# One more PE tap group, a bias table sent from POOL's queue, splits ahead of squares and a layer normalisation on PSUM rows, in a two-layer encoder

## The chip, the cores and the metric

One core of one Trainium2 chip. The metric is the device time of one execution in microseconds (us); before the change its median is 2296.82 us over 3 runs. Engines: PE (TensorE) multiplies matrices, DVE (VectorE), ACT (ScalarE) and POOL (GpSimd) work element by element, and SP (SyncE) only issues DMAs. ACT and POOL can issue DMAs too. Each engine takes its instructions in the order of its own queue, and waits at the head of it.

## The reference, cut to what matters

```python
def _conformer_conv(h, w_in, b_in, dw_w, dw_b, ln_g, ln_b, w_out, b_out):
    u = h @ w_in + b_in
    a, gate = jnp.split(u, 2, axis=-1)
    u = a * jax.nn.sigmoid(gate)
    u = _causal_dwconv(u, dw_w, dw_b)            # 31 taps on each channel
    u = jax.nn.silu(_layernorm(u, ln_g, ln_b))   # over the 2048 channels
    return u @ w_out + b_out

def reference(x, ...):                           # x: 256 positions x 2048 channels
    for i in range(2):
        h = _rmsnorm(x, mix_norm[i])
        m = _conformer_conv(h, ...) if i == 0 else _diff_attention(h, ...)
        x = x + m
        h = _rmsnorm(x, ffn_norm[i])
        x = x + _conv_ffn(h, ...)                # up, 3 taps, silu gate, down
    return _rmsnorm(x, final_norm_g)
```

The attention adds to its scores a bias that depends on the distance of key and query through a table of 32 buckets for each of 16 heads, and masks keys of later chunks of 64.

## The kernel before

Channels lie on the 128 partitions, the 256 positions along the free dimension. Every weight arrives as a 512 KB chunk of f32 (`load_w`, L140, SP's queue, 5 buffers), ACT rounds it to a high part (`split_w`, L150, 6 buffers) and DVE or POOL forms the low part (L152, 6 buffers); PE multiplies high and low parts. A list of steps, one chunk each, is run in order (`run`); `ahead` keeps the splits up to four chunks ahead of PE, and `at(d, fn)` emits `fn` d steps later. The order that reaches the engines' queues is not quite that of the text: a scheduler goes through the program with modelled times, and gives an engine whichever instruction is ready, the earliest in the text first. So a wait that the model takes for short can stand ahead of other work on its queue. Inside `manual_schedule` the order of the text is kept.

**Start** (`setup`). The 8 tiles of x are split for the first product (`split_act`, L267 on ACT and L268 on DVE), four weight splits stand between them, and behind each tile its square is added to a sum on DVE (`x_square`, L321). Then `norm_cols` and `norm_rows` make the reciprocal norms (one small POOL instruction, L286; `rstd`, L348).

**Convolution** (`conv_module`). 16 channel tiles, each 4 chunks of `w_in`; from tile 2 on POOL forms all low parts. After a tile's product `post` scales it (L436, PSUM to an SBUF tile E), ACT takes the sigmoid (L438), DVE makes the gated u (L440). ACT sends u to DRAM (`ud`, L452) and fetches it back in four shifted copies R (L456). On PE, `taps` does the first 4*G taps of the channel with R and diagonals that POOL builds (`dg`, L458; G is 2 groups for tiles 0 to 10, 3 for 11 and 12, 5, 6 and 0 for the last ones); it is emitted 4 steps behind `post`. DVE does the other taps one by one (`tap_step`, L513, at most 6 a step), and `dev` (L544) takes the deviation; POOL sums deviations and squares (L559, L560), for tile 13 DVE. The last tile has 18 taps on PE out of its own tile (`last_taps`, L484) with diagonals built at the start (L466, POOL).

**Layer normalisation** (`layernorm`, in front of the first step of `w_out`). The statistics become two rows (`rows`, L280, in PSUM) which ACT copies to SBUF (L599); DVE (pairs 0, 1, 3, 5, 7) and POOL (2, 4, 6) multiply and subtract them in place (L607, L608, L611), ACT applies Silu (L615) and rounds (L617), DVE forms the low part (L621), and PE starts on `w_out` pair by pair.

**Bias table** (`attn_setup`, emitted at the first step of the first feed-forward part). A small product gives the bias of each head and distance (L730, 16 partitions), and a DMA from ACT's queue writes it 128 times into DRAM (`d1`, L732, 3 MB). In the attention each head's 128x256 window of it is fetched by ACT (`bias`, L809) and masked by POOL (L810). The norm of the first feed-forward part (L285 DVE, L286 POOL, L280 PE, L348 ACT) is emitted just behind `attn_setup`.

Of the kernel before, what the change touches and what calls it, by code (L numbers as in the profile page):

```python
# [8 lines left out]
F32 = mybir.dt.float32  # L9
# [52 lines left out]
class Builder:  # L62
# [79 lines left out]
    def split_w(self):  # L142
# [9 lines left out]
        eng.tensor_tensor(lo[:, :n], raw[:, :n], hi[:, :n].bitcast(F32), ALU.subtract)  # L152
# [42 lines left out]
    def step(self, src, n, cols, mm, post=None, pre=None, lo="v"):  # L195
# [4 lines left out]
        self.steps.append(dict(w=wi, mm=mm, post=post, pre=pre))  # L200

# [177 lines left out]
    def setup(self, n0):  # L379
# [46 lines left out]
    def conv_module(self, nin, nout):  # L426
# [6 lines left out]
        def post(i, ps):  # L433
            with self.tc.high_priority():
                t = self.b2("E")
                nc.vector.tensor_tensor(t, ps[:, :, 0:S], nin["rstd"].unsqueeze(1).to_broadcast([P, 2, S]), ALU.mult)  # L436
# [20 lines left out]
            dg = self.ph1.tile([P, 4 * gm, 32], F32, tag="dg", name=self.nm("dg"))[:, :4 * g, :]  # L457
            nc.gpsimd.tensor_tensor(dg, self.cmask.unsqueeze(1).to_broadcast([P, 4 * g, 32]),  # L458
                                    self.col("wq", 4 * sum(c.G[:i]), 4 * g).unsqueeze(2).to_broadcast([P, 4 * g, 32]), ALU.mult)
            self.at(4, lambda: taps(i, u, R, dg))  # L460
# [78 lines left out]
        def dev(i, acc, rest=None):  # L539
# [7 lines left out]
            if i < KT - 2:  # L547
# [4 lines left out]
                eng = nc.gpsimd if i < KT - 3 else nc.vector  # L552
# [25 lines left out]
        def layernorm():  # L578
# [21 lines left out]
            bc = [rs[:, x, :].unsqueeze(1).to_broadcast([P, 2, S]) for x in range(2)]  # L600
            pools = [pr for pr in range(2, KT // 2) if pr % 2 == 0]

            def norm(pr, part):
                d = D[pr][1]
                if pr == 0:
                    d = d[:, part, :]
                    nc.vector.tensor_tensor(d, d, rs[:, 0, :], ALU.mult)  # L607
                    nc.vector.tensor_tensor(d, d, rs[:, 1, :], ALU.subtract)  # L608
                    return
                eng = nc.gpsimd if pr in pools else nc.vector  # L610
                eng.tensor_tensor(d, d, bc[part], ALU.mult if part == 0 else ALU.subtract)  # L611
# [7 lines left out]
            def low(i):  # L619
                h = hh[i][1]  # L620
                nc.vector.tensor_tensor(h[:, 1, :], D[i // 2][1][:, i % 2, :], h[:, 0, :].bitcast(F32), ALU.subtract)  # L621

            with self.tc.manual_schedule(engines={ET.DVE, ET.Activation, ET.Pool}):
                dve = [pr for pr in range(KT // 2) if pr not in pools]
                todo = [(pr, part) for pr in dve for part in range(2)]
                for x in todo[:2]:
                    norm(*x)
                todo = todo[2:]
                for pr in pools:
                    norm(pr, 0)  # L630
                    norm(pr, 1)
                for i in range(KT):

                    while todo and 2 * todo[0][0] + todo[0][1] <= i + 2:
                        norm(*todo.pop(0))
                    act(i)
                    if todo and i >= 1:
                        norm(*todo.pop(0))
                    low(i)
# [8 lines left out]
        for pr in range(KT // 2):  # L648
            def post2(ps, pr=pr):
                self.x_add(ps, pr, bias="bout")  # L650
                self.x_done(nout, pr)
                if pr == KT // 2 - 1:
                    self.free(hh.values())
                    self.norm_later(nout)
            off = self.pair(a["w_out"], off, c.kcs, lambda k: hh[k], post2, pre=layernorm if pr == 0 else None,
                            lo="g" if pr < 2 else "v")

# [61 lines left out]
    def attn_setup(self):  # L719
# [4 lines left out]
        nc.scalar.dma_start(rb, a["relb"])  # L724
        oh = self.b2("Z").rearrange("p a s -> p (a s)")[:NB, :384]
        nc.scalar.dma_start(oh, a["oneh"])
# [22 lines left out]
    def attention(self, nin, nout):  # L749
# [3 lines left out]
        V, U, O = {}, {}, {}  # L753
# [52 lines left out]
        def bias(h):  # L806
            bm = self.ph2.tile([P, S], F32, tag="bm", name=self.nm("bm"), bufs=2)
            o = h * P * 384 + P - 1
            nc.scalar.dma_start(bm, self.bflat[o:o + P * 383].rearrange("(p d) -> p d", d=383)[:, :S])  # L809
            nc.gpsimd.memset(bm[0:64, S - 64:], MASK)  # L810
            return bm

        def scores(h, q, k, qk):
            bm = bias(h)
# [67 lines left out]
        for h in range(H):  # L882
            if h % 4 == 0:
                voff = v_group(h // 4, voff)
            off = self.pair(a["w_qk"], off, c.kcs, lambda k: nin["xh"][k], lambda ps, h=h: qk_post(h, ps))
# [149 lines left out]
```

## Time and profile before

| | us |
|---|---|
| median of 3 runs (2295.39 to 2298.47) | 2296.82 |
| the profiled execution | 2303.02 |
| its span, first to last instruction | 2300.4 |
| PE busy in the span | 2224.6 |

Names such as L475 are lines of the kernel. `out<-in` names the tiles that an instruction writes and reads. In a timeline the bracket behind an instruction tells how long its engine stood idle before it, and what it waited for. PE's clock has two levels, 1.2 and 2.4 GHz; the profile gives the granted one as a share of the higher.

### The profile page before, as it was taken

To read this page: it belongs to the slowest core of one execution; us is meant where nothing else is said; L and a number is where in the kernel's file an instruction comes from. 1 tells how busy PE (TensorE), PEld (TensorE's weight loads), DVE (VectorE), ACT (ScalarE), POOL (GpSimd) and SP (SyncE) were. 2 spreads that over 40 slices of the span, in tenths; PEclk is the share of its full clock that TensorE was granted. 3 is DMA by queue.
4 is the path that set the end of the run, shared out by engine and by line. 5 is a ranking of instruction groups with operands and counts; after the bars stand their busy time and mean duration, and the time that the engine had idled before them with its cause. 6 is when DMAs were issued, how large, how long until landed. Compare 5 with 4: busy or idle time off the path is not lost.

```text
span 2300.4 us, 34637 instructions
## 1 busy us (share of the span) xinstructions
PE 2224.6 (97%) x13294; PEld 1947.9 (85%) x13294; DVE 1670.9 (73%) x2539; ACT 1205.7 (52%) x1788; POOL 281.4 (12%) x189
## 2 busy tenths in 40 slices
PE   6899799799999999999999999999999999999998
PEld 6788688688888888888888888888888888888887
DVE  5788876577777767677766777677777777676774
ACT  5333265455555555455655555555555555554554
POOL 5678510000000000000111011010000000000002
PEclk9999899899999999999999999999999999999999
DMA  6766356766666666666655555466666666666663
GB/s 230 195 193 190 111 159 179 191 198 187 190 188 188 187 188 190 188 190 188 188 179 159 168 168 166 140 200 183 189 188 190 186 190 185 191 187 190 189 187 100
DMA packets 126885, 417.15 MB, mean 181 GB/s; under 512 B 14176, under 2 KB 28288, under 8 KB 126720
## 3 DMA queue, kind: packets, MB, share of 16 engines
q1 hardware_dynamic: 110736, 398.30, 56.8%
q10 hardware_dynamic: 15984, 16.65, 3.5%
q8 instruction: 104, 1.70, 0.3%
q14 instruction: 61, 0.50, 0.1%
HBM read 407.44 MB, written 7.45 MB: 180 GB/s over the span
## 4 chain that ended last, share of the span: by engine, by line
PE 88%; DMA 5%; DVE 4%; issue 1%; ACTq 0%; ACT 0%; POOL 0%; POOLq 0%; SPq 0%; DVEq 0%
PE pp L226 47%; PE pp L227 24%; PE pp L224 4%; PE pp L217 3%; PE pp L223 2%; DMA R<-ud 2%; DMA ud<-cpad 2%; DMA d<-Z 2%; PE pp L774 1%; PE pp L775 1%; PE pp L776 1%; DVE s L513 1%; DVE cpad L440 1%; PE s L475 0%; ACTq L456 0%
## 5 line engine op out<-in xcount | busy, mean ns | idle before, releaser
L226 PE MATMUL pp<-act,hi 128*128 128x512 f32 x3902 | 1382.9, 396 | 21.1 <-DVE E L256 13.0
L227 PE MATMUL pp<-act,lo 128*128 128x256 f32 x3902 | 1096.5, 281 | 0.0
L150 ACT CAST hi<-raw 128x1024 fp32r<-128x1024 f32 x752 | 787.6, 1049 | 536.0 <-PE pp L226 179.3
L152 DVE TENSOR_TENSOR lo<-raw,hi 128x1024 fp32r<-128x1024 f32 x686 | 844.3, 1231 | 283.0 <-ACT hi L150 281.2
L226 PEld LDWEIGHTS pp<-act,hi 128*128 128x128 f32 x3902 | 733.3, 188 | 182.9 <-DVE E L256 13.3
L227 PEld LDWEIGHTS pp<-act,lo 128*128 128x128 f32 x3902 | 739.1, 189 | 10.4
L226 PE MATMUL pp<-actb,hi 128*128 128x512 f32 x856 | 306.7, 396 | 0.0
L227 PE MATMUL pp<-actb,lo 128*128 128x256 f32 x856 | 240.4, 281 | 0.0
L321 POOL TENSOR_TENSOR ssq<-ssq,Z 128x512 f32<-128x512 f32 x24 | 35.6, 1481 | 1532.1 <-ACT Z L317 1532.0
L217 PE MATMUL pp<-act,hi 128*128 128x256 f32 x1088 | 209.3, 294 | 11.4 <-ACT act L267 6.0
L217 PEld LDWEIGHTS pp<-act,hi 128*128 128x128 f32 x1088 | 178.0, 200 | 19.3 <-DVE act L268 6.6
L226 PEld LDWEIGHTS pp<-actb,hi 128*128 128x128 f32 x856 | 160.6, 188 | 38.3 <-issue 0.6
L152 POOL TENSOR_TENSOR lo<-raw,hi 128x1024 fp32r<-128x1024 f32 x66 | 159.4, 2434 | 56.0 <-ACT hi L150 52.4
L256 DVE TENSOR_TENSOR E<-pp,E 128x512 f32<-128x512 f32 x104 | 71.8, 690 | 128.2 <-ACT E L254 127.9
L227 PEld LDWEIGHTS pp<-actb,lo 128*128 128x128 f32 x856 | 161.5, 189 | 0.2
L217 PE MATMUL pp<-act,lo 128*128 128x256 f32 x544 | 158.4, 291 | 2.8 <-DVE lo L152 2.8
L254 ACT COPY E<-pp 128x512 f32<-128x512 f32 x104 | 60.8, 585 | 186.9 <-PE pp L224 161.6
L370 ACT COPY E<-pp 128x512 f32<-128x512 f32 x109 | 63.9, 586 | 169.5 <-PE pp L224 161.8
L677 DVE SCALAR_TENSOR_TENSOR Y<-fpad,prm,Y 128x256 f32<-128x256 f32 x352 | 146.7, 477 | 0.0
L372 DVE TENSOR_TENSOR x<-pp,x 128x512 f32<-128x512 f32 x101 | 69.7, 690 | 89.4 <-ACT E L370 89.0
L674 ACT ACTIVATE Y<-fpad,prm 128x256 f32<-128x256 f32 x176 | 96.3, 596 | 48.2 <-DVE fpad L670 48.2
L513 DVE SCALAR_TENSOR_TENSOR s<-cpad,cprm,s 128x256 f32<-128x256 f32 x214 | 97.5, 482 | 24.8 <-PE s L475 22.6
(218 smaller groups left out, 1890.8 us busy)
## 6 DMA issues: line engine op xcount, KB each, us to landing
raw<-in_w_up_dram SPq DMA_DIRECT2D x352, 512.0 KB, 4.0
raw<-in_w_down_dram SPq DMA_DIRECT2D x176, 512.0 KB, 4.0
raw<-in_w_in_dram SPq DMA_DIRECT2D x64, 512.0 KB, 4.5
raw<-in_w_qk_dram SPq DMA_DIRECT2D x64, 512.0 KB, 3.6
raw<-in_w_out_dram SPq DMA_DIRECT2D x32, 512.0 KB, 4.1
raw<-in_w_v_dram SPq DMA_DIRECT2D x32, 512.0 KB, 3.7
raw<-in_w_o_dram SPq DMA_DIRECT2D x32, 512.0 KB, 3.7
R<-ud ACTq DMA_DIRECT2D x44, 130.0 KB, 5.1
```

Source lines behind the costliest of these rows:

```text
L150: nc.scalar.copy(hi[:, :n], raw[:, :n])
L152: eng.tensor_tensor(lo[:, :n], raw[:, :n], hi[:, :n].bitcast(F32), ALU.subtract)
L217: nc.tensor.matmul(ps[:, 0:S], w[:, kk, cs], xt[:, x, :], start=(k == first and n == 0), stop=(k == last and n == 2))
L224: nc.tensor.matmul(*main, start=False, stop=True)
L226: nc.tensor.matmul(*main, start=(k == first), stop=False)
L227: nc.tensor.matmul(*corr, start=False, stop=False)
L256: nc.vector.tensor_tensor(t, ps[:, :, 0:S], cs, ALU.add)
L370: nc.scalar.copy(cs, ps[:, :, S:])
L372: nc.vector.tensor_tensor(x, ps[:, :, 0:S], x, ALU.add)
L513: nc.vector.scalar_tensor_tensor(acc, u[:, j:j + S], self.col("cw", i * CK + j), acc, ALU.mult, ALU.add)
L674: nc.scalar.activation(y[:, j, :], u[:, j, FK - 1:], AF.Identity, scale=self.col("fw", ch * FK + FK - 1), bias=self.col("fb", ch))
L677: nc.vector.scalar_tensor_tensor(y[:, j, :], u[:, j, q:q + S], self.col("fw", ch * FK + q), y[:, j, :], ALU.mult, ALU.add)
```

## The change

- `G` becomes 3 for tiles 0 to 12: for tiles 0 to 10 PE does 12 taps in place of 8, DVE 19 in place of 23. `taps` is emitted 5 steps behind `post` for tiles 0 to 13, 4 for tile 14.
- `post` works in place in PSUM: no SBUF tile E, and the PSUM buffer is held until u is made.
- The diagonals of tile 0 and of the last tile are queued on POOL behind the last low part emitted so far.
- `setup` does all splits of x and the first four weight splits, and only then the squares, with two more weight splits between them.
- All sums of deviations and squares go to POOL, two folds for tile 14 also.
- `layernorm`: DVE reads the two rows from PSUM, POOL alone uses the SBUF copy, pair 0 is done by halves first, Silu writes PSUM tiles, and the steps of the first two output pairs alternate.
- `attn_setup`: the three DMAs leave from POOL's queue, and 16 small ones (64 x 64 values each) write the mask into the table behind it. `bias` is fetched from SP's queue, ahead of the head's product, with no masking afterwards.

```diff
-        self.G = [2] * (self.KT - 5) + [3, 3, 5, 6, 0]
+        self.G = [3] * (self.KT - 3) + [5, 6, 0]
...
+    def interleave(self, s0):
+        st = self.steps[s0:]
+        n, w0 = len(st) // 2, st[0]["w"]
+        st = [x for ab in zip(st[:n], st[n:]) for x in ab]
+        self.W[w0:] = [self.W[x["w"]] for x in st]
...
                     self.split_act(n0["xh"][m][1], self.X[pr][:, j, :], self.col("mixg", m))
+
+            for pr in range(KT // 2):
+                if pr % 3 == 2:
+                    self.ahead(4 + pr // 3)
                 self.x_square(n0, pr, nc.vector)
...
-                t = self.b2("E")
-                nc.vector.tensor_tensor(t, ps[:, :, 0:S], nin["rstd"].unsqueeze(1).to_broadcast([P, 2, S]), ALU.mult)
+                t = ps[:, :, 0:S]
+                nc.vector.tensor_tensor(t, t, nin["rstd"].unsqueeze(1).to_broadcast([P, 2, S]), ALU.mult)
...
+            queue = self.tc.issue_after(self.pool_lo) if i == 0 else ExitStack()
+            with queue:
+                diagonals(i, g, dg)
+            self.at(5 if i < KT - 2 else 4, lambda: taps(i, u, R, dg))
...
-                eng = nc.gpsimd if i < KT - 3 else nc.vector
+                eng = nc.gpsimd
...
-                    nc.vector.tensor_tensor(h[x], src[:, 0, :], src[:, 1, :], ALU.add)
+                    nc.gpsimd.tensor_tensor(h[x], src[:, 0, :], src[:, 1, :], ALU.add)
...
+            rp = [self.psx("s", [P, S]) for _ in range(2)]
             rs = self.b2("E")
             for x, v in enumerate((rc, mr)):
-                ps = self.psx("s", [P, S])
-                self.rows(ps, v)
-                nc.scalar.copy(rs[:, x, :], ps)
+                self.rows(rp[x], v)
...
+                if j is not None:
+                    nc.vector.tensor_tensor(d[:, j, :], d[:, j, :], rp[part], ops[part])
+                elif pr in pools:
+                    nc.gpsimd.tensor_tensor(d, d, rs[:, part, :].unsqueeze(1).to_broadcast([P, 2, S]), ops[part])
+                else:
+                    nc.vector.tensor_tensor(d, d, rp[part].unsqueeze(1).to_broadcast([P, 2, S]), ops[part])
...
             def act(i):
-                z = D[i // 2][1][:, i % 2, :]
-                nc.scalar.activation(z, z, AF.Silu, scale=self.col("lng", i), bias=self.col("lnb", i))
+                z = self.psx("to"[i % 2], [P, S])
+                nc.scalar.activation(z, D[i // 2][1][:, i % 2, :], AF.Silu, scale=self.col("lng", i),
+                                     bias=self.col("lnb", i))
...
+                for j in range(2):
+                    norm(0, 0, j)
+                    norm(0, 1, j)
+                for x in range(2):
+                    nc.scalar.copy(rs[:, x, :], rp[x])
...
+            if pr == 1:
+                self.interleave(s0)
...
-        nc.scalar.dma_start(rb, a["relb"])
+        nc.gpsimd.dma_start(rb, a["relb"])
...
-        nc.scalar.dma_start(d1, tb.unsqueeze(1).to_broadcast([H, P, 384]))
+        nc.gpsimd.dma_start(d1, tb.unsqueeze(1).to_broadcast([H, P, 384]))
         self.bflat = d1.rearrange("h p d -> (h p d)")
+
+        mk = self.ph2.tile([64, 64], F32, name="mk")
+        nc.gpsimd.memset(mk, MASK)
+        for h in range(H):
+            o = h * P * 384 + P - 1
+            nc.gpsimd.dma_start(self.bflat[o:o + 64 * 383].rearrange("(p d) -> p d", d=383)[:, S - 64:S], mk)
...
         def bias(h):
-            bm = self.ph2.tile([P, S], F32, tag="bm", name=self.nm("bm"), bufs=2)
+            BM[h] = self.ph2.tile([P, S], F32, tag="bm", name=self.nm("bm"), bufs=2)
             o = h * P * 384 + P - 1
-            nc.scalar.dma_start(bm, self.bflat[o:o + P * 383].rearrange("(p d) -> p d", d=383)[:, :S])
-            nc.gpsimd.memset(bm[0:64, S - 64:], MASK)
-            return bm
+            d = nc.sync.dma_start(BM[h], self.bflat[o:o + P * 383].rearrange("(p d) -> p d", d=383)[:, :S])
+            self.tc.keep_in_program_order(d)
```

## Rows read from the trace of the kernel before

**Rows 1.** PE's waits, whole span: who waited for whom, us, times, longest.
```profile
PE s L475 <- DMA R<-ud: 14.0, 7, 4.9
PE pp L226 <- DVE E L256: 13.0, 1, 13.0
...
PE t L475 <- DMA R<-ud: 6.0, 3, 2.6
...
PE s L484 <- DVE cpad L440: 3.8, 1, 3.8
```

**Rows 2.** Stretches: length, then busy time of PE, PEld, DVE, ACT, POOL, clock, DMA.
```profile
450.00:1150.00 700.00, 700.00 (x4007) 613.16 (x4006) 519.99 (x694) 386.64 (x527) 10.49 (x7) 1.00 0.63 190
```

**Rows 3.** DVE's timeline at the start: start, us, operation.
```profile
30.45 1.21 DVE L152 TENSOR_TENSOR lo<-raw,hi 128x1024 fp32r<-128x1024 f32 x1
```

**Rows 4.** POOL's timeline at the start.
```profile
38.27 14.56 POOL L152 TENSOR_TENSOR lo<-raw,hi 128x1024 fp32r<-128x1024 f32 x6
```

**Rows 5.** DVE's timeline, `post` of tiles 3 and 14: L436 starts as their product ends.
```profile
79.83 0.68 DVE L436 TENSOR_TENSOR E<-pp,rstd 128x512 f32<-128x512 f32 x1
...
239.51 0.68 DVE L436 TENSOR_TENSOR E<-pp,rstd 128x512 f32<-128x512 f32 x1
```

**Rows 6.** The chain that ended last, tiles 11 to 13: start, us, what.
```profile
195.81 0.59 DVE E L436
...
198.63 1.10 PE s L475 x16
...
201.20 5.07 DMA ud<-cpad
...
207.67 5.00 DMA R<-ud
...
212.80 1.50 PE t L475 x24
214.30 11.72 PE pp L217 x96
```

**Rows 7.** POOL's groups, first 300 us: busy us, mean ns, idle before.
```profile
L152 POOL TENSOR_TENSOR lo<-raw,hi 128x1024 fp32r<-128x1024 f32 x66 | 159.4, 2434 | 56.0 <-ACT hi L150 52.4 <-DMA raw<-in_w_in_dram 3.6
...
L560 POOL TENSOR_TENSOR lnsq<-lnsq,Z 128x512 f32<-128x512 f32 x5 | 6.4, 1287 | 0.0
...
L458 POOL TENSOR_TENSOR dg<-cmask,cprm 128x384 f32<-128x384 f32 x2 | 1.9, 928 | 0.0
```

**Rows 8.** DVE's timeline, end of the convolution and layer normalisation.
```profile
257.06 2.60 DVE L568 TENSOR_TENSOR M<-act 128x256 f32<-128x256 f32 x1
...
262.07 0.68 DVE L436 TENSOR_TENSOR E<-pp,rstd 128x512 f32<-128x512 f32 x1
...
280.56 1.48 DVE L607 TENSOR_TENSOR act<-act,E 128x256 f32<-128x256 f32 x1
...
288.71 0.41 DVE L621 TENSOR_TENSOR act<-act,act 128x256 fp32r<-128x256 f32 x1
```

**Rows 9.** PE's timeline around the layer normalisation.
```profile
277.66 1.16 PE L280 MATMUL s<-ident,c 128*128 128x128 f32 x8 [1.51 <-POOL c L593]
286.56 0.80 PE L226 MATMUL pp<-act,hi 128*128 128x512 f32 x1 [7.75 <-DVE act L621]
```

**Rows 10.** ACT's timeline: a Silu, and the start of the feed-forward part.
```profile
288.23 0.60 ACT L615 ACTIVATE act<-act,prm 128x256 f32<-128x256 f32 x1 [3.71 <-DVE act L611]
...
427.82 0.59 ACT L254 COPY E<-pp 128x512 f32<-128x512 f32 x1 [25.08 <-DMA d<-Z]
```

**Rows 11.** POOL's and PE's timelines there.
```profile
400.90 0.70 POOL L286 TENSOR_TENSOR rc<-c,mhalf 128x2 f32<-128x2 f32 x1 [25.41 <-DVE c L285]
...
404.97 0.61 PE L280 MATMUL o<-ident,rc 128*128 128x128 f32 x4
```

**Rows 12.** Weight loads issued from 390 to 430 us: count, landing min/median/max.
```profile
L140 SPq DMA_DIRECT2D raw<-in_w_up_dram x5: 327/2642/4511, 390.9 to 404.7; - x5
...
DMA to landing us min/median/max: 4.5/18.2/18.7
```

More of the change, by code (lines that the diff above doesn't have):

```diff
@@ L151, in split_w @@
         eng = nc.gpsimd if w["lo_eng"] == "g" else nc.vector
-        eng.tensor_tensor(lo[:, :n], raw[:, :n], hi[:, :n].bitcast(F32), ALU.subtract)
+        ins = eng.tensor_tensor(lo[:, :n], raw[:, :n], hi[:, :n].bitcast(F32), ALU.subtract)
+        if w["lo_eng"] == "g":
+            self.pool_lo = ins.ins
         w["hi"] = hi[:, :n].rearrange("p (k c) -> p k c", c=w["cols"])
@@ L200, in step @@
         self.steps.append(dict(w=wi, mm=mm, post=post, pre=pre))
+    def interleave(self, s0):
[3 more added lines that the diff above has]
+        self.W[w0:] = [self.W[x["w"]] for x in st]
+        for i, x in enumerate(st):
+            x["w"] = w0 + i
+        self.steps[s0:] = st
     def pair(self, wsrc, off, ksub, src, post, lo="v", pre=None, held=None, merged=False, halves=None):
@@ L457, in post, with diagonals @@
             dg = self.ph1.tile([P, 4 * gm, 32], F32, tag="dg", name=self.nm("dg"))[:, :4 * g, :]
+            queue = self.tc.issue_after(self.pool_lo) if i == 0 else ExitStack()
+            with queue:
+                diagonals(i, g, dg)
+            self.at(5 if i < KT - 2 else 4, lambda: taps(i, u, R, dg))
+        def diagonals(i, g, dg):
             nc.gpsimd.tensor_tensor(dg, self.cmask.unsqueeze(1).to_broadcast([P, 4 * g, 32]),
                                     self.col("wq", 4 * sum(c.G[:i]), 4 * g).unsqueeze(2).to_broadcast([P, 4 * g, 32]), ALU.mult)
-            self.at(4, lambda: taps(i, u, R, dg))
             if i == 0:
@@ L594, in layernorm @@
             nc.vector.tensor_tensor(mr, mean, rc, ALU.mult)
+            rp = [self.psx("s", [P, S]) for _ in range(2)]
             rs = self.b2("E")
             for x, v in enumerate((rc, mr)):
-                ps = self.psx("s", [P, S])
-                self.rows(ps, v)
-                nc.scalar.copy(rs[:, x, :], ps)
-            bc = [rs[:, x, :].unsqueeze(1).to_broadcast([P, 2, S]) for x in range(2)]
+                self.rows(rp[x], v)
             pools = [pr for pr in range(2, KT // 2) if pr % 2 == 0]
-            def norm(pr, part):
+            ops = (ALU.mult, ALU.subtract)
@@ L604, in norm @@
+            def norm(pr, part, j=None):
                 d = D[pr][1]
[L605 to L611, printed above, removed]
+                if j is not None:
[4 more added lines that the diff above has]
+                    nc.vector.tensor_tensor(d, d, rp[part].unsqueeze(1).to_broadcast([P, 2, S]), ops[part])
@@ L613, in act @@
             def act(i):
-                z = D[i // 2][1][:, i % 2, :]
-                nc.scalar.activation(z, z, AF.Silu, scale=self.col("lng", i), bias=self.col("lnb", i))
+                z = self.psx("to"[i % 2], [P, S])
+                nc.scalar.activation(z, D[i // 2][1][:, i % 2, :], AF.Silu, scale=self.col("lng", i),
+                                     bias=self.col("lnb", i))
                 hh[i] = self.act_tile()
                 nc.scalar.copy(hh[i][1][:, 0, :], z)
-            def low(i):
+                return z
@@ L620, in low @@
+            def low(i, z):
                 h = hh[i][1]
-                nc.vector.tensor_tensor(h[:, 1, :], D[i // 2][1][:, i % 2, :], h[:, 0, :].bitcast(F32), ALU.subtract)
+                nc.vector.tensor_tensor(h[:, 1, :], z, h[:, 0, :].bitcast(F32), ALU.subtract)
             with self.tc.manual_schedule(engines={ET.DVE, ET.Activation, ET.Pool}):
-                dve = [pr for pr in range(KT // 2) if pr not in pools]
-                todo = [(pr, part) for pr in dve for part in range(2)]
@@ L631, in layernorm @@
                     norm(pr, 1)
+                todo = [(pr, part) for pr in range(1, KT // 2) if pr not in pools for part in range(2)]
                 for i in range(KT):
[L634 to L639, printed above, removed]
+                    z = act(i)
+                    for _ in range(2 if i == 1 else 1 if i > 1 else 0):
+                        if todo:
+                            norm(*todo.pop(0))
+                    low(i, z)
             self.free(D.values())
@@ L752, in attention @@
         H, KT = c.H, c.KT
-        V, U, O = {}, {}, {}
+        V, U, O, BM = {}, {}, {}, {}
         def v_group(g, off):
@@ L884, in attention @@
                 voff = v_group(h // 4, voff)
-            off = self.pair(a["w_qk"], off, c.kcs, lambda k: nin["xh"][k], lambda ps, h=h: qk_post(h, ps))
+            off = self.pair(a["w_qk"], off, c.kcs, lambda k: nin["xh"][k], lambda ps, h=h: qk_post(h, ps),
+                            pre=lambda h=h: bias(h))
         off = 0
```

9 lines of the change are left out of this document (4 added, 5 removed).

## The prediction

> **What bounds the kernel now.** I read PE's waits over the whole span first, because PE is busy 2224.6 of 2300.4 us (the table above): whatever is to be won without less work lies in the other 76 us. Four causes that this change touches make 36.8 of them [rows 1]: PE stands for the shifted copies R in front of its taps, 14.0 and 6.0 us in ten waits, so 2.0 on average; once for 13.0 us behind DVE's scaling in the first feed-forward part; and 3.8 us in front of the last tile's taps. Next, the stretches: from 450 to 1150 us PE is busy for all of 700.00 us at the full clock [rows 2], so nothing can be won there, and the change can only disturb it. What counts is the first 430 us. There I read DVE and POOL at the start [rows 3, 4], the ends of tiles 3 and 14 [rows 5], the chain of one tile [rows 6], POOL's load [rows 7], the end of the convolution [rows 8, 9], and ACT, POOL, PE and the weight loads around the bias table [rows 10 to 12].
>
> **The start, up to the end of tile 3.** Tile 1's first weight chunk gets its low part on DVE only at 30.45 [rows 3], behind the squares, and PE waits for it. With the squares last, x is split some 10 us earlier, and the chunk follows. But tile 2 needs POOL's low parts, which begin at 38.27 [rows 4], and POOL now builds the diagonals just ahead of them, so I don't let them begin earlier. Four of 2.434 each [rows 7] end at 48.0; a last chunk of 2.93 (a quarter of 11.72, [rows 6]) ends tile 2 at 50.9; taps and tile 3, 1.50 + 11.72 [rows 6], give 64.1 in place of 79.83 [rows 5]: 15.7 at most. Against it, R of tile 0 hangs on the norm, which still waits for the squares. If the norm came no earlier, only the later place of the taps would be won, one chunk of 2.93. The whole of either is unlikely; I take 10, from 3 to 15.7.
>
> **Tiles 3 to 14.** Now they take 239.51 - 79.83 = 159.7 us [rows 5], 14.52 each. PE's own work in a tile is 11.72, and its taps 1.10 with two groups and 1.50 with three [rows 6]. So the third group costs PE 0.40 a tile, and takes four taps from DVE. What makes 12.8 into 14.5 is the round trip of u: from the end of tile 11's product at 195.81 to the landing of R at 212.67 it takes 16.9 us, of which two transfers are 5.07 and 5.00 [rows 6]; PE reaches the taps one tile later and waits. Two things shorten the wait. The taps stand one chunk later, 13.22 + 2.93 = 16.2 us behind the product. And the trip loses its DVE delays: in tile 11 DVE stood behind the taps of tile 10, which PE did at 198.63 [rows 6], before it could make u. After the change these taps come behind u in the text. Scaling, sigmoid and u at about 0.6 each, the transfers and some 1.5 for four issues make about 13.4, within 16.2. So the period falls to PE's own 13.22, and 11 x (14.52 - 13.22) = 14.3. I take 13, as transfers differ. If transfers are 4 us slower than these two, 1.2 a tile of wait is left, and of 14.3 some 1; so from 1 to 14.3. POOL must keep up: four low parts, one set of diagonals and half of two sums, 4 x 2.434 + 0.928 + 1.287 [rows 7], are 11.95 of 13.22 us. It fits, with 1.3 to spare.
>
> **The last tile.** Tile 15's scaling begins at 262.07, behind DVE's sums, of which a single 128x256 one took 2.60 [rows 8]. These go to POOL. PE's 3.8 us in front of the last taps [rows 1] should go, and one more wait for R, 2.0: 5.8, from 2 to 7. POOL gets the two folds; they are needed by the fold of tile 14, at the end of some ten microseconds of DVE taps, which covers them; without that cover they cost about 2 x 1.3 [rows 7].
>
> **The layer normalisation.** The rows begin on PE at 277.66, and `w_out` starts at 286.56, having waited 7.75 for the first low part [rows 9]. In between a DVE multiply took 1.48 while POOL was busy, where a pass of the same 128x256 took 0.41 with POOL idle [rows 8]. After the change DVE reads one operand from PSUM, needs no copy by ACT first, and does half a pair: 278.4 (the rows' end) + 2 x 0.41 + Silu 0.60 [rows 10] + rounding and low part 2 x 0.41 + handing over 0.4 = 281.0. That wins 5.5, from 3 to 6: the low part of the first channel may still meet POOL. The interleaved pairs win nothing more, I think; PE's work there is the same and four chunks are split ahead.
>
> **The bias table.** ACT stood 25.08 us until the 3 MB table had landed [rows 10], since the fetch of the first head's bias was queued in front of its copy of a finished product; PE ran dry 13.0 of these [rows 1]. With the fetch on SP in the attention's own place, ACT has no such wait, and the 13.0 go. The queues it passes: SP fetches a head's window between weight loads; its buffer is freed by a head two before, so nothing much waits there. POOL gets four instructions and 16 mask writes, which wait for the table; behind them, or ahead of them, is the small norm instruction, done at 400.90, which PE's rows at 404.97 need [rows 11]. Everything hangs on this order. In the modelled times the fetches of the bias, ready when the table had landed, were placed on ACT's queue in front of the copy, but the norm stood first on POOL; I expect the norm first, and the masks behind it with nothing else queued for hundreds of us. Value 13.0; from -51 to 13.0 (below).
>
> The trace shows a second effect of this transfer: loads of weights issued at the time took 18.2 us, where the shortest took 4.5 [rows 12]. The Trainium skill, "DMA: Bandwidth & Descriptors", section "Issuing engines are not separate DMA queues", says that DMAs of all issuing engines run on the same 16 engines, and another queue saves only the issue time. By that rule the loads stay 13.7 late. With four chunks of 2.93 split ahead, that would leave PE waiting 2, and the sum would be 45.3 in place of 47.3.
>
> **The sum.** 10 + 13 + 5.8 + 5.5 + 13.0 = 47.3. The profiled execution took 2303.0, a span of 2300.4 and 2.6 around it; it would become 2255.7. It lies 6.2 above the median, and I take the gain from the median: 2296.8 - 47.3 = 2249.5.
>
> **Rivals.**
> *POOL or ACT becomes the bound of the convolution.* POOL has only 1.3 us a tile to spare [rows 7], and ACT stands still while it waits for `ud`. If the period becomes 14.0, tiles win 11 x 0.52 = 5.7, and the start loses 4 of its 10: 36 in all, 2260.8. For it: POOL's queue gets everything; against it: low parts are formed well ahead of PE now, and POOL waited 52.4 us for ACT [rows 7].
> *The change doesn't do what it says for the table*: another wait for the same transfer keeps the 13.0. Gain 34.3, 2262.5.
> *The masks stand ahead of the norm on POOL.* The table lands at about 427 [rows 10], 16 issues of at least 0.33 [rows 12] and the norm 0.70 follow: 433. PE, which reaches the rows at 404.97 [rows 11], waits 28 in place of 13. Gain 34.3 - 15 = 19.3, 2277.5.
> *Slower: that order, with a slower table.* Sent from POOL while weights flow, the transfer may take twice its 35 us; the norm would come at 468, PE would wait 63, 50 more than now, and 50 - 34.3 make the kernel 15.7 slower: 2312.5. It decides from a norm later than 452 on. The Trainium skill, "SBUF — State Buffer", section "SBUF: two separate sides", warns that a DMA of POOL's queue gets its descriptors from POOL's cores, which DVE can lock out; no row here shows such a DMA.
>
> **How the numbers follow.** Forecast 0.62; POOL or ACT the bound 0.16; table wait kept 0.07; masks first 0.07; masks first and slow 0.05; a disturbed order elsewhere that eats the gain 0.03. The terms' own ends reach from 25 to 56 of gain; a further few can come from PE's clock, where fewer waits leave it at its higher level. So the range is 2237 to 2270, which holds the forecast and the first two rivals. A measurement of this kernel tells a change of about 0.2%, 4.6 us. Faster: 0.93; same 0.02; slower 0.05.
>
> **What would show it.** In the changed profile: tile 3's product ends near 70 and tile 14's near 213; PE's waits for R fall from 20.0 to under 5; the last taps follow tile 14's without a gap; PE starts `w_out` about 8 us behind its last taps; no wait of PE between 390 and 430, and the norm on POOL ahead of the mask writes. I'd be wrong if PE now waits for POOL's low parts, if R is waited for as before, or if PE stands in front of the norm's rows.

## The result, and the profile after

| | before | after |
|---|---|---|
| median of 4 runs, us | 2297.64 | 2268.32 (2265.20 to 2270.85) |
| profiled execution / its span | 2303.02 / 2300.4 | 2268.81 / 2267.0 |
| ratio of the medians, 95% interval | | 0.9873 [0.9856, 0.9890] |

The kernel became 29.3 us faster. The forecast was 2249.5 us, a gain of 47.3; the measured time lies near the upper end of its range of 2237 to 2270. The direction was right and the size was 18 us off, so the question is where those went.

First PE's waits over the whole span (who waited for whom, us in total, times, longest):

```profile
PE o L292 <- POOL rc L298: 11.7, 2, 10.7
...
PE pp L238 <- DVE act L645: 3.1, 1, 3.1
PE pp L238 <- DVE E L268: 2.8, 1, 2.8
PE pp L229 <- DVE cpad L457: 2.2, 1, 2.2
...
PE pp L238 <- ACT hi L150: 1.7, 1, 1.7
...
PE t L498 <- DMA R<-ud: 1.4, 1, 1.4
...
PE s L498 <- DMA R<-ud: 1.2, 1, 1.2
...
PE pp L239 <- DVE lo L152: 0.8, 1, 0.8
```

Against [rows 1]: the waits for R fell from 20.0 to 2.6 us, the 13.0 behind the blocked copy and the 3.8 in front of the last taps are gone. New is the first line: 10.7 us in one piece for a norm on POOL. The lines `E L268`, `hi L150` and `lo L152` are three small waits at about 400 us.

The marks, as in [rows 5]: DVE's timeline with the scaling of tiles 3, 14 and 15.

```profile
83.85 0.69 DVE L453 TENSOR_TENSOR pp<-pp,rstd 128x512 f32<-128x512 f32 x1
...
227.13 0.70 DVE L453 TENSOR_TENSOR pp<-pp,rstd 128x512 f32<-128x512 f32 x1 [0.96 <-PE pp L229]
241.12 0.70 DVE L453 TENSOR_TENSOR pp<-pp,rstd 128x512 f32<-128x512 f32 x1 [2.53 <-PE pp L229]
```

PE's timeline around the layer normalisation, to be read beside [rows 9]:

```profile
257.36 1.66 PE L292 MATMUL s<-ident,c 128*128 128x128 f32 x8 [1.52 <-POOL c L616]
262.11 0.80 PE L238 MATMUL pp<-act,hi 128*128 128x512 f32 x1 [3.09 <-DVE act L645]
```

From these marks the gain can be split as the prediction split it:

| stretch, worked out from marks of both traces | forecast | measured |
|---|---|---|
| start to tile 3's mark: 79.83 - 83.85 | 10 (3 to 15.7) | -4.0 |
| tiles 3 to 14: 159.68 - 143.28 | 13 (1 to 14.3) | 16.4 |
| tile 14's mark to the rows: 38.15 - 30.23 | 5.8 (2 to 7) | 7.9 |
| rows to `w_out`: 8.90 - 4.75 | 5.5 (3 to 6) | 4.15 |
| around the table | 13.0 (-51 to 13) | 7.2 |
| the rest | 0 | 1.7 |
| sum, of spans | 47.3 | 33.4 |

The table's 7.2 is the change of lead between two copies of finished products on ACT: 310.46 - 285.76 = 24.7 ahead of it, 446.60 - 414.70 = 31.9 behind it. Two terms failed, the start by 14.0 us and the table by 5.8. Tiles 3 to 14 and the last tile were better than forecast, by 3.4 and 2.1, and the layer normalisation was 1.35 short. 33.4 is a difference of two spans of profiled executions. Before's execution was 5.4 above its median and after's 0.5, and the time outside the span fell from 2.6 to 1.8 us; that leads from 33.4 to the 29.3 of the medians.

**The start.** DVE's, POOL's and PE's timelines:

```profile
35.53 0.16 DVE L297 TENSOR_SCALAR c<-o 128x2 f32<-128x2 f32 x1 [0.70 <-PE o L286]
```
```profile
30.70 5.03 POOL L489 TENSOR_TENSOR Y<-ident,cprm 128x512 f32<-128x512 f32 x4
...
37.06 11.54 POOL L152 TENSOR_TENSOR lo<-raw,hi 128x1024 fp32r<-128x1024 f32 x5
48.56 0.68 POOL L298 TENSOR_TENSOR rc<-c,mhalf 128x2 f32<-128x2 f32 x1
```
```profile
49.30 1.23 PE L292 MATMUL o<-ident,rc 128*128 128x128 f32 x4 [10.71 <-POOL rc L298]
52.75 0.79 PE L229 MATMUL pp<-act,hi 128*128 128x256 f32 x2 [2.22 <-DVE cpad L457]
```

The input of the norm is ready at 35.7, when DVE's L297 ends. Before the change POOL made the norm in front of tile 2's low parts, which followed at 38.27 [rows 4]:

```profile
37.61 0.69 POOL L286 TENSOR_TENSOR rc<-c,mhalf 128x2 f32<-128x2 f32 x1 [7.38 <-DVE c L285]
```

Now five low parts come first, and a 0.68 us instruction waits 13 us in a queue. PE has finished two tiles by 38.6 and stands. Its granted clock suffers too (two stretches: length, busy PE, PEld, DVE, ACT, POOL, clock, DMA):

```profile
38.60:46.55 7.95, 0.00 (x0) 0.00 (x0) 0.00 (x0) 1.04 (x1) 7.95 (x5) 0.50 0.52 178
46.55:67.03 20.48, 14.34 (x110) 13.23 (x110) 5.89 (x12) 4.26 (x6) 9.92 (x6) 0.76 0.62 173
```

**The tiles.** PE, which idled 11.8 of 142.4 us between tiles 4 and 14 before, is busy for the whole stretch now:

```profile
95.73:227.13 131.40, 131.40 (x1202) 122.55 (x1201) 107.32 (x222) 48.26 (x56) 115.55 (x61) 1.00 0.74 213
```

Each tile takes 13.14 us, its product and its taps and nothing else, as the chain shows:

```profile
126.28 11.71 PE pp L229 x96
137.99 1.43 PE s L498 x24
139.42 11.71 PE pp L229 x96
```

**The table.** POOL's timeline, then the landing of the five weight loads issued beside the transfer:

```profile
366.55 1.03 POOL L759 DMA_DIRECT2D d<-Z  x1 [15.28 <-DVE Z L757]
375.81 0.71 POOL L298 TENSOR_TENSOR rc<-c,mhalf 128x2 f32<-128x2 f32 x1 [8.23 <-DVE c L297]
404.29 1.11 POOL L766 DMA_DIRECT2D d<-mk  x2 [27.77 <-DMA d<-Z]
```
```profile
DMA to landing us min/median/max: 22.7/26.4/28.6
```

The norm stands ahead of the masks, as forecast, and PE doesn't wait for it. But the loads took 22.7 to 28.6 us, against 18.2 in the median before [rows 12], and PE ran dry 5.3 us (2.8 + 1.7 + 0.8) between 400 and 408.

### The profile page after: what moved, and what is told of

Same layout as the page of the kernel before. It is cut to its first block, busy times and chain, and to the rows that moved or that the text cites. A ratio compares the mean times of both kernels' runs of the same rounds, so it can differ in the third digit from the quotient of the medians.

```text
span 2267.0 us, 34768 instructions
## 1 busy us (share of the span) xinstructions
PE 2219.3 (98%) x13382; PEld 1944.0 (86%) x13382; DVE 1635.4 (72%) x2491; ACT 1205.2 (53%) x1788; POOL 292.0 (13%) x197
## 4 chain that ended last, share of the span: by engine, by line
PE 94%; DMA 2%; DVE 1%; POOL 0%; ACT 0%; issue 0%; ACTq 0%; POOLq 0%; DVEq 0%
PE pp L238 48%; PE pp L239 25%; PE pp L229 7%; PE pp L236 4%; PE pp L235 2%; PE pp L807 1%; PE pp L809 1%; PE pp L808 1%; DMA raw<-in_w_up_dram 1%; PE s L498 1%; DMA R<-ud 0%; PE o L292 0%; PE s L854 0%; DMA ud<-cpad 0%; PE t L498 0%; PE o L286 0%
## 5 line engine op out<-in xcount | busy, mean ns | idle before, releaser
L150 ACT CAST hi<-raw 128x1024 fp32r<-128x1024 f32 x752 | 788.0, 1049 | 529.2 <-PE pp L238 180.9
L152 DVE TENSOR_TENSOR lo<-raw,hi 128x1024 fp32r<-128x1024 f32 x686 | 846.0, 1234 | 301.0 <-ACT hi L150 299.0
L239 PEld LDWEIGHTS pp<-act,lo 128*128 128x128 f32 x3902 | 741.1, 190 | 10.3
L333 POOL TENSOR_TENSOR ssq<-ssq,Z 128x512 f32<-128x512 f32 x24 | 35.6, 1483 | 1516.6 <-ACT Z L329 1516.5
L229 PE MATMUL pp<-act,hi 128*128 128x256 f32 x1088 | 203.4, 289 | 9.1 <-ACT act L279 6.2
L152 POOL TENSOR_TENSOR lo<-raw,hi 128x1024 fp32r<-128x1024 f32 x66 | 158.3, 2414 | 57.6 <-ACT hi L150 52.1
L268 DVE TENSOR_TENSOR E<-pp,E 128x512 f32<-128x512 f32 x104 | 71.8, 691 | 105.1 <-ACT E L266 104.9
L229 PEld LDWEIGHTS pp<-act,lo 128*128 128x128 f32 x544 | 106.7, 196 | 2.1 <-POOL lo L152 1.7
```

The source lines that it names most:

```text
L150: nc.scalar.copy(hi[:, :n], raw[:, :n])
L152: ins = eng.tensor_tensor(lo[:, :n], raw[:, :n], hi[:, :n].bitcast(F32), ALU.subtract)
L229: nc.tensor.matmul(ps[:, 0:S], w[:, kk, cs], xt[:, x, :], start=(k == first and n == 0), stop=(k == last and n == 2))
L239: nc.tensor.matmul(*corr, start=False, stop=False)
L268: nc.vector.tensor_tensor(t, ps[:, :, 0:S], cs, ALU.add)
```

## The experiments

The chips of these runs were a little slower: the kernel before took 2302.0 to 2303.1 us beside them. So ratios of medians to it are given, to be compared with 0.9873 for the change, and spans and marks of the traces, which are of one execution each. The four executions of e1 range from 2254.31 to 2262.62 us, and its trace is of one of 2254.84; a difference of a few us between two spans counts only where the marks show where it arises. In kernels with the first edit, line numbers are two higher.

### The start: is it the norm's place on POOL?

**e1_norm_first.**

```diff
-        self.nc.gpsimd.tensor_tensor(dst, v, self.mhalf, ALU.pow)
+        self.rc_ins = self.nc.gpsimd.tensor_tensor(dst, v, self.mhalf, ALU.pow).ins
...
+        behind = self.tc.issue_after(self.rc_ins) if i == 8 else ExitStack()
+        with behind:
             ins = eng.tensor_tensor(lo[:, :n], raw[:, :n], hi[:, :n].bitcast(F32), ALU.subtract)
```

> The changed kernel with one edit: the low part of chunk 8 (the first of tile 2) is queued on POOL behind the small instruction that makes the first norm, so no low part of tile 2 stands in front of it. Theory A, the norm's place on POOL's queue cost the start: in the changed kernel the norm's input is ready at 35.7 us but POOL makes the norm at 48.56, behind five low parts. Then here the norm comes at about 37.5, PE's wait of 10.7 us for it shrinks to about 1, tile 2's product begins near 42 in place of 52.75, and after some 2 us lost in front of the first taps the time is 8 to 11 us less: about 2258. Rival B, the scaling in place holds both product buffers in PSUM until u is made, and that delays tile 2 whatever the norm does: the wait only changes its name, and the time stays within 2 us of 2268.

Measured: 0.9815 [0.9794, 0.9837], span 2253.0, 14.0 us under the changed kernel's. POOL's and PE's timelines, and the stretch after the norm:

```profile
36.75 0.69 POOL L300 TENSOR_TENSOR rc<-c,mhalf 128x2 f32<-128x2 f32 x1
```
```profile
41.38 0.51 PE L231 MATMUL pp<-act,hi 128*128 128x256 f32 x2 [2.22 <-DVE cpad L459]
```
```profile
46.55:67.03 20.48, 19.78 (x188) 18.06 (x187) 12.41 (x29) 6.56 (x7) 18.55 (x11) 1.00 0.93 275
```

The norm comes 11.8 us earlier, tile 2's product 11.4, and tile 3's mark is at 70.22 in place of 83.85, 13.6. That is more than expected, with the clock at its higher level in that stretch, where it was granted 0.76 before this edit. Theory A holds. The held buffer (the 2.22 us behind `cpad`) stays at 2.2 and is not the cause.

**e2_diag_early.**

```diff
-            queue = self.tc.issue_after(self.pool_lo) if i == 0 else ExitStack()
-            with queue:
-                diagonals(i, g, dg)
+            diagonals(i, g, dg)
```

> The changed kernel, but the diagonals of tile 0 and of the last tile are not queued behind the low parts emitted so far; POOL makes them from about 17 us on, as in the kernel before. The norm still stands behind five low parts of tile 2 in POOL's order. Theory A (what counts is when POOL comes to the norm): the seven low parts begin some 5 us earlier, the norm is made at about 43 in place of 48.6, and the time falls by about 5, to 2263. If instead the early diagonals slow DVE's splits as much as they free POOL (DVE's two-input SBUF operations took 3 times as long beside POOL in the kernel before), tile 1's product ends later than 38.6 and the time stays at 2268.

Measured: 0.9852 [0.9833, 0.9872], span 2266.7, the changed kernel's. POOL and DVE:

```profile
26.58 18.98 POOL L152 TENSOR_TENSOR lo<-raw,hi 128x1024 fp32r<-128x1024 f32 x7 [0.98 <-ACT hi L150]
45.52 0.69 POOL L298 TENSOR_TENSOR rc<-c,mhalf 128x2 f32<-128x2 f32 x1
```
```profile
30.18 5.71 DVE L333 TENSOR_TENSOR ssq<-ssq,Z 128x512 f32<-128x512 f32 x2
...
44.45 0.16 DVE L297 TENSOR_SCALAR c<-o 128x2 f32<-128x2 f32 x1 [1.11 <-PE o L286]
```

By the ratio it is 0.002 lower, within the intervals, and tile 3's mark comes 0.9 us earlier. The second answer was right in its outcome, though the sums of squares were slowed more than the splits. POOL came 3 us sooner to the norm, but now its input was late: DVE's sums of squares took 2.9 us each beside a POOL that never rests, where before the change single ones took 0.68 with POOL idle, and c came at 44.45 in place of 35.53. With the squares last, queueing the diagonals late was sound.

**e3_old_setup.**

```diff
-            for pr in range(KT // 2):
-                if pr % 3 == 2:
-                    self.ahead(4 + pr // 3)
                 self.x_square(n0, pr, nc.vector)
```

> The changed kernel with the start of the kernel before: each square stands behind its own splits again, and no weight splits are moved. In this order the norm stands ahead of tile 2's low parts on POOL. Theory A: the squares' place is what pushed the norm behind the low parts, so undoing it wins: the norm comes at about 38, tile 3's product ends near 76 in place of 83, and the time is about 2261, though behind the kernel with the norm forced first (2258), since the splits of x come later. Rival B (the buffers, not the norm): tile 3's product ends at 82 or later, and the time is 2268 to 2272.

Measured: 0.9803 [0.9789, 0.9818], span 2257.0. Undoing this part of the change wins 10 us of span:

```profile
33.59 0.83 POOL L478 TENSOR_TENSOR dg<-cmask,cprm 128x384 f32<-128x384 f32 x1
34.38 0.69 POOL L298 TENSOR_TENSOR rc<-c,mhalf 128x2 f32<-128x2 f32 x1
35.04 11.71 POOL L152 TENSOR_TENSOR lo<-raw,hi 128x1024 fp32r<-128x1024 f32 x5
```

With the squares among the splits the norm stands in front of the low parts; with the squares last, and two more weight splits between them, behind five of them. So it was this reordering that put the norm late; the squares and the two weight splits were not parted. The norm's input is ready at 28.4 here, so it still waits 6 us on POOL, now behind the diagonals alone.

With the norm in front in both, tile 3's mark is at 74.04 here and at 70.22 in e1. But the squares' place doesn't bring the start of tile 2 forward: PE begins it at 38.06 here, 3.3 us ahead of e1, and loses this afterwards, as it stands for R of tile 0:

```profile
38.06 0.50 PE L229 MATMUL pp<-act,hi 128*128 128x256 f32 x2 [2.22 <-DVE cpad L453]
50.75 2.79 PE L494 MATMUL s<-R,dg 128*32 128x256 f32 x24 [4.24 <-DMA R<-ud]
```

From 50 to 60 us the granted clock is then 0.69, in e1 1.00. The times of e1 and e3 don't tell them apart.

### The table: the engines or the queue?

**e4_table_spread.**

```diff
-        nc.gpsimd.dma_start(d1, tb.unsqueeze(1).to_broadcast([H, P, 384]))
+        def piece(x, n=32):
+            r = P // n
+            d = nc.sync.dma_start(d1[:, x * r:(x + 1) * r, :], tb.unsqueeze(1).to_broadcast([H, r, 384]))
+            self.tc.keep_in_program_order(d)
...
+        for x in range(32):
+            self.at(1 + x, lambda x=x: piece(x))
+        self.at(34, masks)
```

> The changed kernel, with the 3 MB table sent not as one transfer from POOL's queue but as 32 pieces from SP's queue, one behind each weight load's step, over about 95 us; the masks follow at the end. Theory C, the transfer starves the weight loads beside it: in the changed kernel loads issued from 370 to 385 us take 22.7 to 28.6 us to land, and PE waits about 5.3 us between 380 and 410. Then here loads keep landing within 8 us, PE has no wait in that stretch, and the time is about 5 less: 2263. Rival D, the loads are slow because of something else at this place (the switch from w_out to w_up, or SP's issue): PE's waits stay at 3 us or more, and the time stays at 2268.

Measured: 0.9826 [0.9811, 0.9840], span 2258.3, 8.7 less, of which 1.2 are there by 285 us. The 32 weight loads issued from 365 to 460 us landed as if no table were sent, and PE has no wait in the stretch:

```profile
DMA to landing us min/median/max: 3.5/4.6/5.3
```

So PE's 5.3 us came from the transfer beside the loads, and with them a granted clock of 0.83 from 408 to 418 us, where e4 has 1.00 from 400 to 445.

**e8_table_act**, on e1: the table's three DMAs back to ACT's queue.

```diff
-        nc.gpsimd.dma_start(rb, a["relb"])
+        nc.scalar.dma_start(rb, a["relb"])
...
-        nc.gpsimd.dma_start(oh, a["oneh"])
+        nc.scalar.dma_start(oh, a["oneh"])
...
-        nc.gpsimd.dma_start(d1, tb.unsqueeze(1).to_broadcast([H, P, 384]))
+        nc.scalar.dma_start(d1, tb.unsqueeze(1).to_broadcast([H, P, 384]))
```

> e1_norm_first, but the three DMAs of the table leave from ACT's queue, as before the change; the masks stay on POOL and the fetches on SP. Theory C, the transfer takes the shared DMA engines from the weight loads whatever queue it leaves from: loads issued beside it still land after 18 us or more, PE still waits 3 to 6 us in that stretch, and the span is within 3 us of e1's. Rival: POOL's queue is what starves the loads (22.7 to 28.6 us in the changed kernel, against 16.5 to 18.7 with ACT's queue in the kernel before): PE's waits fall under 2 us and the span is 3 us or more below e1's.

Measured: 0.9766 [0.9741, 0.9790], span 2247.1, 5.9 under e1, with no wait of PE in the stretch, where e1 has 3.9 us. The rival was right and my theory C wrong: the same 3 MB in 36.7 us, from a single DMA, cost PE nothing. The five loads beside it landed in

```profile
DMA to landing us min/median/max: 14.2/17.9/18.9
```

The queues' shares while both flow (packets, MB, share of the 16 engines), first the changed kernel from 386 to 402 us, then e8 from 374 to 388:

```profile
q0 software_dynamic: 330, 1.46, 79.4%
q1 hardware_dynamic: 355, 1.32, 20.2%
```
```profile
q10 hardware_dynamic: 818, 1.26, 58.1%
q1 hardware_dynamic: 662, 2.38, 42.0%
```

The weights are q1. Beside POOL's queue (q0) they moved 1.32 MB in 16 us, beside ACT's (q10) 2.38 MB in 14. The two queues moved packets in like numbers in either case, but those of POOL's queue hold 4.4 KB (1.46 MB / 330) and those of ACT's 1.5 KB. That engines take turns packet by packet would explain it; no run here varied the packet size alone.

**e5_both**, e1 and e4 together.

> The norm queued first on POOL (as in e1_norm_first) and the table sent in 32 pieces from SP's queue (as in e4_table_spread) together. If the two losses are independent, their gains add: e1's span was 14.0 us and e4's 8.7 us under that of the changed kernel, so the span becomes about 2244.5, and the ratio to the kernel before about 0.977. If they share a cause (the clock's low stretches, or a wait that one edit only hands to the other), the sum falls short by 4 us or more.

Measured: 0.9769 [0.9749, 0.9789], span 2246.7, 20.3 under the changed kernel's where the two gains add to 22.7; 1.2 of e4's lay ahead of the table. The sum falls short by less than the 4 us set beforehand, so the losses count as independent.

### The tiles: which edit won?

**e6_at4**, on e1:

```diff
-            self.at(5 if i < KT - 2 else 4, lambda: taps(i, u, R, dg))
+            self.at(4, lambda: taps(i, u, R, dg))
```

> e1_norm_first, but the taps on PE stand 4 steps behind the scaling again, as before the change, still with 3 groups. Theory: the later place is what removed the waits for R. In e1 the trip from a tile's mark to the landing of R takes 13.2 to 15.2 us, 14.4 on the mean of tiles 3 to 13, and taps stood some 16 us behind the mark; one chunk earlier, at 13.1, they would wait about 1.2 us a tile: tiles 3 to 14 take about 157 us in place of 145, and the span is about 10 us more than e1's. Rival: the trip itself became short enough (u is no longer behind DVE's taps), and the place does nothing: within 3 us of e1.

Measured: 0.9831 [0.9806, 0.9856], span 2262.4, 9.4 above e1. Tiles 3 to 14 take 151.6 in place of 145.0, and PE's wait is back:

```profile
PE s L500 <- DMA R<-ud: 6.3, 4, 2.4
```

The later place is worth 6.6 us in the tiles, where 12 were expected: the trip took 12.9 us on the mean here (tiles 4 to 13), not 14.4. The span came out as expected all the same; by the marks 0.8 us arise in front of tile 3 and 2 behind tile 14.

**e7_two_groups**, on e1:

```diff
-        self.G = [3] * (self.KT - 3) + [5, 6, 0]
+        self.G = [2] * (self.KT - 5) + [3, 3, 5, 6, 0]
```

> e1_norm_first, but tiles 0 to 10 have 2 groups of taps on PE and 23 taps on DVE again, still 5 steps behind. Theory: with the wait for R gone PE's own work sets the period, so the third group only costs: the period of tiles 3 to 10 falls from 13.14 to about 12.75, some 3 to 4 us in all, and the span falls by as much. Rival: DVE becomes the bound. It is busy for 10.8 of 13.14 us in the changed kernel; four more taps of 0.4 us each make 12.4 of 12.75, so u comes later behind them, R is waited for, and the last tile finds a backlog of taps: the span is 3 us or more above e1's.

Measured: 0.9771 [0.9746, 0.9795], span 2247.6, 5.4 under e1. The stretch from tile 5 to tile 14:

```profile
94.97:210.00 115.03, 115.03 (x1025) 108.23 (x1024) 100.07 (x232) 43.20 (x50) 104.38 (x56) 1.00 0.80 219
```

PE is still busy throughout, at 12.70 us for a tile with two groups, and DVE for 100.07 of 115.03 us. The rival, DVE as the bound, doesn't occur. The third group, the first thing the change names, costs 0.44 us a tile and wins nothing once the taps stand a chunk later. By the marks 5.0 us are won at tile 14 and 3.7 at the first output pair; the rest of the 5.4 arises behind it.

**e11_post_sbuf**, on e1:

```diff
-                t = ps[:, :, 0:S]
-                nc.vector.tensor_tensor(t, t, nin["rstd"].unsqueeze(1).to_broadcast([P, 2, S]), ALU.mult)
+                t = self.b2("E")
+                nc.vector.tensor_tensor(t, ps[:, :, 0:S], nin["rstd"].unsqueeze(1).to_broadcast([P, 2, S]), ALU.mult)
```

> e1_norm_first, but the scaling of a tile's product writes an SBUF tile again and u is made from that, as before the change. Theory: the making of u then reads two operands from SBUF and takes 1.4 us in place of 0.49 while POOL works; the trip from mark to R grows from 14.4 to about 15.3 us, still within the 16.1 that the taps leave, so the span is 0 to 3 us above e1's. PE's wait of 2.2 us in front of tile 2, for the buffer that is held until u is made, shrinks by some 1 us. Rival: the held buffer matters more than that, and the span falls by 2 us or more.

Measured: 0.9830 [0.9810, 0.9851], span 2262.8, 9.8 above e1: far more than expected. DVE's making of u between 60 and 230 us, here and in e1 (count, busy us, mean ns, idle before):

```profile
L459 DVE SCALAR_TENSOR_TENSOR cpad<-E,prm,G 128x256 f32<-128x256 f32 x13 | 22.9, 1763 | 2.4 <-ACT G L457 2.4
```
```profile
L459 DVE SCALAR_TENSOR_TENSOR cpad<-pp,prm,G 128x256 f32<-128x256 f32 x12 | 5.8, 479 | 0.0
```

The trip from the mark to the landing of R is 15.4 us on the mean of tiles 4 to 13, as expected, against 14.4 in e1; but it reaches 17.1, and PE waits 7.4 us for R in six places. The expectation went by the mean; the waits are made by the longest trips. By the marks 1.3 us arise in front of tile 3, 4.3 from there to tile 14 and 3.7 from tile 14 to the first output pair.

### Two smaller parts, and all together

**e9_no_interleave**, on e1, the `interleave` call taken out.

> e1_norm_first, but the steps of the first two output pairs follow one another instead of alternating. Theory, as in the prediction: PE's work behind the layer normalisation is the same and four chunks are split ahead, so the alternation wins nothing; the second pair's product ends within 1 us of e1's and the span is within 2 us of 2253. Rival: the alternation hides the normalisation of later channels (a pair needs all 16 of them at once, two pairs need each only half as fast): PE waits for the low parts of later channels, 2 to 4 us in all.

Measured: 0.9814 [0.9793, 0.9835], span 2256.5. Ahead of the layer normalisation it is 0.5 us behind e1, at the first output pair 1.6. So the alternation is worth about 1 us; the other 2 us of the span arise near the table, where PE's longest wait (`pp` for DVE's E) is 3.4 us here, 1.3 in e1 and 2.8 in e10, whose table is sent the same way.

**e10_sums_dve**, on e1, the sums of tile 13 and the two folds back on DVE.

> e1_norm_first, but the sums for tile 13 and the two folds for tile 14 are done by DVE again. Theory: these sums, 2.2 to 2.9 us each beside a busy POOL in the kernel before, stood in front of the last tile's scaling; with them back, tile 15's mark comes 3 to 6 us later than e1's 229.18 and the span grows by as much. Rival: DVE has some 16% free time now that it does fewer taps, and the sums fall into it: tile 15's mark stays within 1 us, and so does the span within 2.

Measured: 0.9815 [0.9794, 0.9836], span 2257.2. Tile 15's mark comes 15.4 us behind tile 14's, in e1 14.0; by the first output pair 2.1 are lost. That lies between the two answers: the two sums and two folds take DVE 5.5 us, and its free time takes in over half of them. One fold took 0.41 us, the other 1.99, beside a low part on POOL that ran from 230.79 to 233.44:

```profile
230.79 0.41 DVE L593 TENSOR_TENSOR M<-act 128x256 f32<-128x256 f32 x1
231.13 0.69 DVE L455 TENSOR_TENSOR pp<-pp,rstd 128x512 f32<-128x512 f32 x1
231.73 1.99 DVE L593 TENSOR_TENSOR M<-lnsq 128x256 f32<-128x256 f32 x1
```

**e12_best**: norm first, two groups, table from ACT's queue.

> e1_norm_first with 2 groups of taps (e7) and the table from ACT's queue (e8). The spans of e7 and e8 were 5.4 and 5.9 us under that of e1. One acts on tiles 3 to 12, the other on the stretch around 390 us, so the gains should add: a span of about 2241.7, a ratio to the kernel before of about 0.972, and no wait of PE over 1.5 us between 60 and 230 us or between 340 and 420 us. If less than 8 us under e1 remains, one of the two gains was the other's.

Measured: 2245.12 us, 0.9752 [0.9735, 0.9768], span 2242.7, 10.3 under e1, where the two gains add to 11.3. It beats both kernels: 57.9 us under the kernel before beside it. PE's one wait between 60 and 420 us that is over 1.5 us is the 3.1 in front of `w_out`; tile 3's mark lies at 68.65, tile 14's at 209.65.

## Why the prediction was right, and where it was wrong

**The start: wrong, and in its sign.** The step that failed is "if the norm came no earlier, only the later place of the taps would be won": the case of a norm that comes later was left out, and with it any loss, so the lower end of 3 had no reason. The norm came at 48.56 in place of 37.61. The step in front of it held in its outcome: DVE's splits of x end at 18.2 us in place of 28.0, some 10 earlier, and PE ended two tiles at 38.6.

```profile
24.69 3.34 DVE L268 SCALAR_TENSOR_TENSOR act<-x,prm,act 128x256 fp32r<-128x256 f32 x2
```
```profile
16.55 1.67 DVE L280 SCALAR_TENSOR_TENSOR act<-x,prm,act 128x256 fp32r<-128x256 f32 x4
```

But it gave this to the squares alone. With the squares among the splits and the diagonals late the splits end at 20.7 (e3), with the squares last and the diagonals early at 20.5 (e2): either edit wins most of the 10. The norm is an instruction on POOL, and the text had POOL building diagonals and four low parts just there; where the norm would stand among them wasn't asked. The same question was asked of the second norm at the table, and there the order was right. e1 and e3 show the cause from two sides: tile 3's mark comes 13.6 us earlier with the norm put first, and 9.8 with the squares put back, though PE then waits for R of tile 0. With the norm first, the forecast's 10 becomes 79.83 - 70.22 = 9.6; the 10 was taken between two ends and not worked out, so that is luck in part.

**Tiles 3 to 14: right, and a little low.** The trip was put at 13.4 us and the place at 16.2; over tiles 4 to 13 the trip measures 13.4 on the mean (12.6 to 14.1). So R is there, and PE's own 13.14 (forecast 13.22) sets the period. 1.2 of the 16.4 come from the marks, as tile 3's mark lies 1.3 us behind the end of its product at 82.55. The reasons were only half named: u in place took 0.48 us, and e11 shows that this is as much a condition of the short trip as the order of the queue. That the third group costs 0.40 a tile was right (0.44 in e7); the forecast took its help to DVE as the other side of that, and e7 shows that DVE didn't need it.

**The last tile and the layer normalisation: right.** 7.9 for 5.8, of which e10 gives some 2 to the sums on POOL; the rest wasn't taken apart. 4.15 for 5.5: the rows took 1.66 us, where the sum had put their end 0.74 behind their start, though [rows 9] gives 1.16, and from there to `w_out` it took 3.1, not 2.6. The alternation wins 1 us where none was forecast.

**The table: the mechanism right, the price of its side effect too low.** ACT's wait and PE's 13.0 went, and the masks stood behind the norm. But the 3 MB cost the loads more from POOL's queue than from ACT's, 26.4 us in the median for 18.2, and PE 5.3 us. The forecast had this as a sentence beside the sum, with 2 us, and left it out of the 47.3. The Trainium skill, "DMA: Bandwidth & Descriptors", section "Issuing engines are not separate DMA queues", as it was used there (another queue saves the issue time and no more), names the effect, since loads suffered under both queues; but by it e8 should have equalled e1, and it is 5.9 us shorter. Here the measurement differs from the rule. That DVE holds up the descriptors of POOL's queue (the Trainium skill, "SBUF — State Buffer", section "SBUF: two separate sides") doesn't show: the transfer took 37.5 us here and 36.3 in e1, against 35.6 in the kernel before and 36.7 in e8 from ACT's queue.

**The rivals.** POOL as the bound of the convolution didn't come: POOL was busy for 115.55 of 131.40 us and PE for all of it. The table's wait came back in part, by another way. "The masks ahead of the norm" and its slow form didn't occur, though the mechanism, a short instruction that PE needs behind a queue of long ones, did, at the other norm.

**The sum.** Of the 18.8 us between forecast and result, 13.9 lie in the terms, by spans. Of the other 5, some 4 come from reading the terms in an execution that was itself 5.4 above its median, and 0.8 from the median of the kernel before, which a fourth run moved from 2296.82 to 2297.64; where the 5.4 lay can't be told from one trace. Three of the five terms fell outside their own ends, the start below, tiles 3 to 14 (16.4 for at most 14.3) and the last tile (7.9 for at most 7) above. That the time lies in the range is owed in part to their making up for each other. And the terms' lower ends, with the table won, add up to 22 and not to 25.

## What to carry to other kernels

A wait that is taken off the end of a queue is won only if the small instruction that releases the next stage doesn't slide behind bulk work on another queue: for each instruction that PE needs, look up who stands ahead of it after the edit, and allow a loss in the bound where you don't know. When several edits go in together, take each out again once: here one that cost 4 to 5 us (the third group) and one that, with the norm left behind the low parts, cost 10 (the squares last) hid behind those that won. And price a transfer by what it does to the loads beside it, by queue, and a chain with slack by its longest trips, not by their mean.

## What the hardware showed that was not expected

- One 3 MB DMA with the same source and target left in packets of 4.4 KB from POOL's queue and of 1.5 KB from ACT's. Beside the former the weights got 20.2% of the engines' time, beside the latter 42.0%.
- At the start of the transfer the loads got nothing from either queue: for 11 us of each (370 to 381 in the changed kernel, 359 to 370 in e8) the engines moved the table alone, at 97 to 98 GB/s, with several loads issued. Why is open.

```profile
q0 software_dynamic: 234, 1.08, 98.7%
```
```profile
q10 hardware_dynamic: 695, 1.07, 93.0%
```

- The same bytes in 32 pieces behind the weight loads, on their own queue, slowed none of them: 4.6 us in the median (e4).
- A DVE instruction on 128x256 with two SBUF operands took 1.76 us on the mean beside POOL, 0.48 with one of them in PSUM (e11 and e1).
